# One probability tile per head, V products by key block, and the softmax sums inverted late and sent through DRAM

## The chip, the cores and the metric

The kernel runs on one core of a Trainium2 chip. The metric is the device time of one execution in microseconds (us), lower is better. The engines are named as in the profile: PE (TensorE matmul), PEld (its weight loads), DVE (VectorE), ACT (ScalarE), POOL (GpSimd) and SP (SyncE, which here issues all DMAs of the program from one queue, in order).

## The reference

Two layers over 2048 tokens of width 1024, all float32. Layer A is a gated MLP with spatial gating. Layer B, which the change touches, is chunked band attention with 16 heads of 64 channels: a chunk of 64 queries sees its own chunk and the 8 chunks before it.

```python
def one_chunk(args):
    c, qc = args
    start = c * CHUNK
    kc = lax.dynamic_slice_in_dim(k_pad, start, B_BAND, axis=1)
    vc = lax.dynamic_slice_in_dim(v_pad, start, B_BAND, axis=1)
    sc = jnp.einsum('bqhd,bkhd->bhqk', qc, kc).astype(jnp.float32) + bias
    valid = (m + start) >= B_LEFT_PAD
    sc = jnp.where(valid[None, None, None, :], sc, NEG_INF)
    p = jax.nn.softmax(sc, axis=-1).astype(vc.dtype)
    return jnp.einsum('bhqk,bkhd->bqhd', p, vc)
...
return (o * jax.nn.silu(z)) @ w_out
```

## The kernel before

Matmuls keep float32 accuracy by splitting each operand into a high part, rounded to float32r, and a low part, the rest; a product is two or three matmuls (`mm3`, lines 113 to 115, for the dense layers).

Layer A and the projection of V come first. The attention layer B runs from about 1560 us of the span to the end. It has four token tiles `t` of 512 queries, and in each eight pairs `p` of heads. A head has four query blocks of 128 queries (`qb`), so a pair has eight units, `u` = 0 to 7: head `hd` = u // 4 of the pair, block u % 4. A query block sees five key blocks of 128 keys, 640 keys, in the tiles `t` > 0; in the first tile the keys before the sequence are left out, so it sees 1, 2, 3 or 4 blocks.

A unit goes through three functions:

- `score`: four matmuls (line 1320) into one PSUM tile; DVE adds the bias, negates, and leaves the row minimum (line 1328, tile `pr`); ACT takes the exponential and leaves the row sum in `sl` (line 1335); DVE inverts `sl` (line 1338); POOL multiplies the whole row by it (line 1339).
- `flip`: PE transposes the five blocks of `pr` into the one PSUM tile `tp` (line 1359); ACT copies them as the high part (line 1362) and DVE writes the low part (line 1363) into `pt`. One `pt` tile holds two query blocks side by side, for each of six key blocks: [128, 2 (high, low), 6, 256]. In the first token tile POOL writes zeros into the corner that no block fills (line 1352).
- `value`, once for two query blocks (`g`): the products with V. The stationary operand is a block of V for one head, 64 columns of its high part and 64 of its low part; the moving operand is `pt`, 256 columns at a time. For `t` > 0 there are ten matmuls: eight for the four key blocks that both query blocks see (line 1387), high and low, and one each for the outermost key blocks, in which high and low of one query block stand side by side (lines 1380 and 1381). The two halves of the output are added afterwards: ACT copies one (line 1399), DVE adds the other (line 1401), and for `t` > 0 DVE adds high and low (line 1406). After the last call of a pair DVE multiplies by the gate `zt` (line 1413; for the last two pairs of all `last_og`, line 1486) and the result goes to DRAM.

The order is written out by hand in the loop over `u`, and a scheduler of the framework may still move instructions on each engine within the dependencies. In each step stand: the score of unit u + 2, half of the other work of that step, the flip of unit u, for even u a `value`, and the other half. The other work is a generator (`ahead`): the projection of the next pair (query, key and gate: `pj` tiles), and the output product of the tile before (`bo` tiles). The output product of the last tile stands alone at the end. In the first token tile the projection weights are scaled by the norm gains on POOL (line 184) before ACT and DVE split them (lines 199 and 200). In tiles 0, pairs 2 and 4, POOL also forms sums of the output weights (lines 310 to 319).

The PSUM tiles `tp` and the score tile have one buffer each. SP's queue carries all loads and stores, the shift of the query tiles by 64 partitions (`Qh<-Qh`) among them.

Of the kernel before, what the change touches and what calls it, by code (L numbers as in the profile page):

```python
# [9 lines left out]
F32 = mybir.dt.float32  # L10
F32R = mybir.dt.float32r
# [22 lines left out]
def trunk_kernel(  # L34
# [43 lines left out]
    x2d = [[dram.tile([P, D], F32, name=f"x2d{t}_{b}") for b in range(TB)] for t in range(NT - 1)]  # L78

# [1127 lines left out]
    with ExitStack() as bctx:  # L1207
# [83 lines left out]
        prs = {}  # L1291
        pts = {}
# [12 lines left out]
        def score(t, p, u):  # L1305
# [12 lines left out]
            for i, q in enumerate(qt[t, p, hd]):  # L1318
# [8 lines left out]
            sl = sm.tile([P, 1], F32, tag="sl", name=f"sl{t}_{h}_{qb}", bufs=4)  # L1327
# [8 lines left out]
                pr[:, c0:], pr[:, c0:], AF.Exp, scale=-1.0, bias=nm[:], accum_out=sl[:]  # L1336
            )
            nc.vector.reciprocal(sl[:], sl[:])  # L1338
            nc.gpsimd.tensor_scalar(  # L1339
                pr[:, c0:], pr[:, c0:], sl[:], 1.0, op0=ALU.mult, op1=ALU.mult  # L1340
            )
            prs[t, h, qb] = pr

        def flip(t, p, u):

            hd, qb = divmod(u, 4)
            h = 2 * p + hd
            g, qq = divmod(qb, 2)
            if qq == 0:
                pt = sb.tile([P, 2, 6, 256], F32R, tag="PT", name=f"pt{t}_{h}_{g}", bufs=2)  # L1350
                if t == 0:
                    nc.gpsimd.memset(pt[:, :, 5, 0:P].bitcast(F32), 0.0)
                pts[t, h, g] = pt
            pt = pts[t, h, g]
            pr = prs[t, h, qb]
            b0 = 0 if t > 0 else 4 - qb
            tp = ptr.tile([P, KD, P], F32, tag="tr", name=f"tp{t}_{h}_{qb}")
            for b in range(b0, 5):
                tpose(tp[:, b, :], pr[:, b * P : (b + 1) * P], ident[:])  # L1359
            cs = slice(qq * P, (qq + 1) * P)  # L1360
            oh = pt[:, 0, b0 + qq : 5 + qq, cs]
            nc.scalar.copy(oh, tp[:, b0:5, :])  # L1362
            nc.vector.tensor_tensor(  # L1363
                pt[:, 1, b0 + qq : 5 + qq, cs], tp[:, b0:5, :], oh.bitcast(F32), op=ALU.subtract
            )

        def value(t, p, hd, g):

            h = 2 * p + hd
            pt = pts[t, h, g]  # L1370
            po = pmm.tile([P, 2, 256], F32, tag="mm", name=f"pv{t}_{h}_{g}")
            hs = slice(hd * P, hd * P + P)

            def keys(i):
                return vtl[t, p][:, 2 * g + i, hs]

            if t > 0:
                mm(po[:, :, 0:P], keys(0), pt[:, :, 0, 0:P], start=True, stop=False)  # L1380
                mm(po[:, :, P:256], keys(5), pt[:, :, 5, P:256], start=False, stop=False)
                blocks = range(1, 5)
            else:
                blocks = range(4 - 2 * g, 6)
            for j in range(2):
                for i in blocks:
                    mm(  # L1387
                        po[:, 0, :], keys(i), pt[:, j, i, :],
                        start=(t == 0 and j == 0 and i == blocks[0]),
                        stop=(j == 1 and i == blocks[-1]),  # L1390
                    )
            if hd == 0 and g == 0:
                og32s[t, p] = sb.tile([P, T], F32, tag="og32", name=f"og32_{t}_{p}", bufs=1)
            og32 = og32s[t, p]
            r, r2 = halves(hd)
            ot = sb.tile([P, 2, 256], F32, tag="ot", name=f"ot{t}_{h}_{g}", bufs=1)
            oq = og32[r, g * 256 : (g + 1) * 256]
            n = 2 if t > 0 else 1
            nc.scalar.copy(ot[r, :n, :], po[r2, :n, :])
            o1 = ot[r, :, :] if t > 0 else oq  # L1400
            nc.vector.tensor_tensor(
                o1, po[r, :n, :] if t > 0 else po[r, 0, :],
                ot[r, :n, :] if t > 0 else ot[r, 0, :], op=ALU.add,
            )
            if t > 0:
                nc.vector.tensor_tensor(oq, ot[r, 0, :], ot[r, 1, :], op=ALU.add)
            if g == 0:
                return
            if hd == 1 and t + 1 == NT and p >= 6:
                last_og(p, og32, zt[t, p])  # L1410
            elif hd == 1:
                og = sb.tile([P, T], F32, tag="og", name=f"og{t}_{p}", bufs=2)
# [220 lines left out]
        for t in range(NT):  # L1633
            for p in range(NPAIR):
# [11 lines left out]
                for u in range(8):  # L1646
# [6 lines left out]
                    done = max(done, upto)  # L1653
                    flip(t, p, u)
# [15 lines left out]
        value(*before, 1, 1)  # L1670
# [61 lines left out]
```

## Time and profile before

| | |
|---|---|
| median of 3 runs | 2727.69 us (2720.04 to 2733.72) |
| the profiled execution, its own time | 2731.61 us |
| its span in the profile | 2728.6 us |
| mean granted TensorE clock | 0.986 |
| PE busy | 2630.1 us, 96% |
| DVE busy | 1961.0 us, 72% |
| ACT busy | 1324.8 us, 49% |
| POOL busy | 909.8 us, 33% |

Busy times of PE overlap, since a matmul starts while the one before it drains: what a matmul costs in a dense stretch is the distance from its start to the next start, which the timeline shows. In the groups of instructions, the number after the bar is idle time of that engine just before the group, with what ended it.

### The profile page before, as it was taken

To read this page: it belongs to the slowest core of one execution; us is meant where nothing else is said; L and a number is where in the kernel's file an instruction comes from. 1 tells how busy PE (TensorE), PEld (TensorE's weight loads), DVE (VectorE), ACT (ScalarE), POOL (GpSimd) and SP (SyncE) were. 2 spreads that over 40 slices of the span, in tenths; PEclk is the share of its full clock that TensorE was granted. 3 is DMA by queue.
4 is the path that set the end of the run, shared out by engine and by line. 5 is a ranking of instruction groups with operands and counts; after the bars stand their busy time and mean duration, and the time that the engine had idled before them with its cause. 6 is when DMAs were issued, how large, how long until landed. Compare 5 with 4: busy or idle time off the path is not lost. (4 is left out here: it accounts for less than half of the span.)

```text
span 2728.6 us, 38857 instructions
## 1 busy us (share of the span) xinstructions
PE 2630.1 (96%) x13216; PEld 2199.9 (81%) x13216; DVE 1961.0 (72%) x3097; ACT 1324.8 (49%) x2360; POOL 909.8 (33%) x906
## 2 busy tenths in 40 slices
PE   8999999999999999999989998999999999999997
PEld 7888888888888888888867776778887888788885
DVE  5655676676676669666677776677788778877787
ACT  5422242433424445332455465566656666666554
POOL 3512236142251414115143344322333223323243
PEclk9999999999999999999999999899999999999999
DMA  7899999989888879668667787766777667865567
GB/s 297 314 326 335 345 358 327 329 306 349 333 300 295 302 263 342 236 236 308 239 219 277 238 274 249 243 211 208 234 253 246 219 211 238 264 203 192 185 228 251
DMA packets 274773, 735.56 MB, mean 270 GB/s; under 512 B 29584, under 2 KB 61328, under 8 KB 274576
## 3 DMA queue, kind: packets, MB, share of 16 engines
q1 hardware_dynamic: 274576, 733.09, 77.9%
q8 instruction: 105, 1.72, 0.3%
q14 instruction: 92, 0.75, 0.1%
HBM read 540.56 MB, written 181.93 MB: 265 GB/s over the span
## 5 line engine op out<-in xcount | busy, mean ns | idle before, releaser
L113 PE MATMUL P<-T,S 128*128 128x512 f32 x1248 | 496.1, 398 | 2.7 <-ACT S L376 2.0
L115 PE MATMUL P<-T,S 128*128 128x512 f32 x1248 | 490.3, 393 | 0.0
L114 PE MATMUL P<-T,S 128*128 128x512 f32 x1248 | 489.1, 392 | 1.1 <-DVE T L379 1.1
L1339 POOL TENSOR_SCALAR pr<-pr,sl 128x640 f32<-128x640 f32 (+4 forms) x256 | 202.8, 792 | 553.9 <-DVE sl L1338 512.8
L113 PE MATMUL pj<-hh_b,wh_b 128*128 128x512 f32 x768 | 316.8, 412 | 7.7 <-ACT wh_b L199 6.7
L114 PE MATMUL pj<-hl_b,wh_b 128*128 128x512 f32 x768 | 307.4, 400 | 0.0
L115 PE MATMUL pj<-hh_b,wl_b 128*128 128x512 f32 x768 | 306.5, 399 | 0.0
L1335 ACT ACTIVATE pr<-pr,nm 128x640 f32<-128x640 f32 (+4 forms) x256 | 195.3, 763 | 222.4 <-DVE nm L1328 217.5
L115 PEld LDWEIGHTS P<-T,S 128*128 128x128 f32 x1248 | 235.4, 189 | 50.3
L113 PEld LDWEIGHTS P<-T,S 128*128 128x128 f32 x1248 | 235.9, 189 | 48.1 <-ACT S L376 2.3
L114 PEld LDWEIGHTS P<-T,S 128*128 128x128 f32 x1248 | 235.8, 189 | 46.9 <-DVE T L379 1.3
L1363 DVE TENSOR_TENSOR pt<-tp,pt 128x640 fp32r<-128x640 f32 (+4 forms) x256 | 188.8, 738 | 75.4 <-ACT pt L1362 73.1
L1328 DVE CUSTOM_DVE_ANT_0 pr<-s,bias 128x640 f32<-128x640 f32 (+4 forms) x256 | 188.2, 735 | 21.4 <-PE s L1320 15.6
L1362 ACT CAST pt<-tp 128x640 fp32r<-128x640 f32 (+4 forms) x256 | 158.6, 620 | 60.8 <-PE tp L1359 58.0
L1359 PEld LDWEIGHTS tp<-ident,pr 128*128 128x128 f32 x1120 | 135.1, 140 | 54.5 <-POOL pr L1339 15.9
L1359 PE MATMUL tp<-ident,pr 128*128 128x128 f32 x1120 | 165.8, 274 | 12.7 <-DVE pt L1363 6.5
L115 PEld LDWEIGHTS pj<-hh_b,wl_b 128*128 128x128 f32 x768 | 147.3, 192 | 32.6
L113 PEld LDWEIGHTS pj<-hh_b,wh_b 128*128 128x128 f32 x768 | 147.7, 192 | 27.5 <-ACT wh_b L199 8.3
L114 PEld LDWEIGHTS pj<-hl_b,wh_b 128*128 128x128 f32 x768 | 147.9, 193 | 17.3 <-issue 0.2
L1387 PE MATMUL pv<-pt,V 128*128 128x256 f32 x960 | 143.0, 289 | 11.2 <-ACT pt L1362 11.1
L200 DVE TENSOR_TENSOR wl_b<-raw_b,wh_b 128x1024 fp32r<-128x1024 f32 x96 | 122.9, 1280 | 42.4 <-ACT wh_b L199 41.2
L1387 PEld LDWEIGHTS pv<-pt,V 128*128 128x128 f32 x960 | 127.5, 193 | 14.9 <-ACT pt L1362 13.6
(291 smaller groups left out, 5941.5 us busy)
## 6 DMA issues: line engine op xcount, KB each, us to landing
S<-hsd SPq DMA_DIRECT2D x288, 512.0 KB, 5.5
rw<-in_w_a SPq DMA_DIRECT2D x108, 512.0 KB, 6.5
A<-ytd SPq DMA_DIRECT2D x72, 512.0 KB, 5.5
raw_b<-wk SPq DMA_DIRECT2D x72, 512.0 KB, 3.8
hsd<-S SPq DMA_DIRECT2D x56, 512.0 KB, 4.3
V<-vhd SPq DMA_DIRECT2D x56, 512.0 KB, 5.0
wh_bo<-ows SPq DMA_DIRECT2D x50, 512.0 KB, 4.5
wl_bo<-ows SPq DMA_DIRECT2D x50, 512.0 KB, 5.6
```

The source lines that it names most:

```text
L113: first = mm(ps, lh, rh, start=first, stop=False)
L114: mm(ps, lh, rl, start=False, stop=False)
L115: mm(ps, ll, rh, start=False, stop=last)
L200: tv(wl[:], raw[:], wh[:].bitcast(F32), op=sub)
L1328: nc.vector.tensor_tensor_reduce(out=pr[:, c0:].rearrange("p (a b) -> p a b", a=nseg), in0=ps[:, :nseg, :w], in1=bias[:, c0:].rearrange("p ...
L1335: nc.scalar.activation(pr[:, c0:], pr[:, c0:], AF.Exp, scale=-1.0, bias=nm[:], accum_out=sl[:])
L1339: nc.gpsimd.tensor_scalar(pr[:, c0:], pr[:, c0:], sl[:], 1.0, op0=ALU.mult, op1=ALU.mult)
L1359: tpose(tp[:, b, :], pr[:, b * P : (b + 1) * P], ident[:])
L1362: nc.scalar.copy(oh, tp[:, b0:5, :])
L1363: nc.vector.tensor_tensor(pt[:, 1, b0 + qq : 5 + qq, cs], tp[:, b0:5, :], oh.bitcast(F32), op=ALU.subtract)
L1387: mm(po[:, 0, :], keys(i), pt[:, j, i, :], start=(t == 0 and j == 0 and i == blocks[0]), stop=(j == 1 and i == blocks[-1]),)
```

## The change

The probabilities are no longer multiplied by the inverse sums. The eight row sums of a pair go into eight columns of one tile; DVE inverts that tile once, after the eighth exponential. PE transposes it, 128 x 8 to 8 x 128, into a free slot of the `tp` tile of unit 6 (unit 5 in the last pair of all). ACT copies the 8 x 128 to SBUF, one DMA writes it to DRAM, two DMAs read it back, each spread over the 64 partitions of a head, and POOL multiplies the result by the gate.

One `pt` tile holds all four query blocks of a head, and has one buffer. `value` is called once for a head and goes by key block: for each of the eight key blocks (four in the first token tile) two matmuls, high and low, over all query blocks that see it, so 128, 256, 384 or 512 columns. High and low are accumulated in one PSUM tile, and the output is read once for a head. `value` of the first head stands ahead of the flip of unit 4, that of the second ahead of the flip of unit 0 of the next pair; the gate and the store follow in `gated`, one step later.

```diff
-            sl = sm.tile([P, 1], F32, tag="sl", name=f"sl{t}_{h}_{qb}", bufs=4)
+            if u == 0:
+                sums[t, p] = sm.tile([P, 8], F32, tag="sl", name=f"sl{t}_{p}", bufs=2)
...
             nc.scalar.activation(
-                pr[:, c0:], pr[:, c0:], AF.Exp, scale=-1.0, bias=nm[:], accum_out=sl[:]
+                pr[:, c0:], pr[:, c0:], AF.Exp, scale=-1.0, bias=nm[:],
+                accum_out=sums[t, p][:, u : u + 1],
             )
-            nc.vector.reciprocal(sl[:], sl[:])
-            nc.gpsimd.tensor_scalar(
-                pr[:, c0:], pr[:, c0:], sl[:], 1.0, op0=ALU.mult, op1=ALU.mult
-            )
+            if u == 7:
+                nc.vector.reciprocal(sums[t, p][:], sums[t, p][:])
...
-                pt = sb.tile([P, 2, 6, 256], F32R, tag="PT", name=f"pt{t}_{h}_{g}", bufs=2)
-                if t == 0:
-                    nc.gpsimd.memset(pt[:, :, 5, 0:P].bitcast(F32), 0.0)
+            if qb == 0:
+                pts[t, h] = sb.tile([P, 5376], F32R, tag="PT", name=f"pt{t}_{h}", bufs=1)
...
             for b in range(b0, 5):
                 tpose(tp[:, b, :], pr[:, b * P : (b + 1) * P], ident[:])
+            if u == sums_at(t, p):
+                tpose(tp[0:8, 5, :], sums[t, p][:], ident[:])
...
+            if u == sums_at(t, p):
+                inverse(t, p, tp[0:8, 5, :])
+
+        def sums_at(t, p):
+            return 5 if t + 1 == NT and p + 1 == NPAIR else 6
+
+        def inverse(t, p, src):
+            rc = sm.tile([8, P], F32, tag="rc", name=f"rc{t}_{p}", bufs=1)
+            nc.scalar.copy(rc[:], src)
+            nc.sync.dma_start(rcd[t][p].rearrange("(a b) -> a b", b=P), rc[:])
+            w = zt[t, p, 1] = sb.tile([P, T], F32, tag="og", name=f"w{t}_{p}", bufs=2)
+            for hd in range(2):
+                nc.sync.dma_start(
+                    w[hd * 64 : hd * 64 + 64, :],
+                    rcd[t][p, hd * T : hd * T + T].partition_broadcast(64),
+                )
+            tg(w[:], w[:], zt[t, p][:], op=ALU.mult)
 
-        def value(t, p, hd, g):
+        def value(t, p, hd):
...
+            blocks = (3, 4, 0, 1, 2, 5, 6, 7) if t > 0 else (4, 5, 6, 7)
+            for i in blocks:
+                q0, q1 = max(0, i - 4), min(4, i + 1)
+                for j in range(2):
+                    o = j * 2560 + q0 * 512 + i * P
+                    rhs = pt[:, o : o + P]
+                    if q1 - q0 > 1:
+                        rhs = pt[:, o : o + (q1 - q0) * 512].rearrange("p (q c) -> p q c", c=512)
+                        rhs = rhs[:, :, 0:P]
                     mm(
+                        po[:, q0 * P : q1 * P], vtl[t, p][:, i, hs], rhs,
+                        start=(i == blocks[0] and j == 0), stop=(i == 7 and j == 1),
                     )
...
+            nc.scalar.copy(ot[r, :], po[r2, :])
+            nc.vector.tensor_tensor(og32[r, :], po[r, :], ot[r, :], op=ALU.add)
+
+        def gated(t, p):
+            og32, og = og32s[t, p], zt[t, p, 1]
+            if t + 1 == NT and p >= 6:
+                last_og(p, og32, og)
+            else:
                 nc.vector.scalar_tensor_tensor(
-                    og[:], og32[:], 0.5, zt[t, p][:], op0=ALU.mult, op1=ALU.mult
+                    og[:], og32[:], 0.5, og[:], op0=ALU.mult, op1=ALU.mult
                 )
...
+                    if u == 1 and before:
+                        gated(*before)
+                    if u == 4:
+                        value(t, p, 0)
+                    elif u == 0 and before:
+                        value(*before, 1)
                     flip(t, p, u)
...
-                    if u % 2 == 0:
-                        if u:
-                            value(t, p, *divmod(u // 2 - 1, 2))
-                        elif before:
-                            value(*before, 1, 1)
...
-        value(*before, 1, 1)
+        value(*before, 1)
+        gated(*before)
```

More of the change, by code (lines that the diff above doesn't have):

```diff
@@ L78, in trunk_kernel @@
     x2d = [[dram.tile([P, D], F32, name=f"x2d{t}_{b}") for b in range(TB)] for t in range(NT - 1)]
+    rcd = [dram.tile([NPAIR, 8 * P], F32, name=f"rcd{t}") for t in range(NT)]
     reld = [dram.tile([P * 768], F32, name=f"reld{h}") for h in range(NH)]
@@ L1291, in trunk_kernel @@
         prs = {}
+        sums = {}
         pts = {}
@@ L1367, in value @@
-        def value(t, p, hd, g):
+                pt[:, 2560 + o + b0 * P : 2560 + o + 640],
+                tp[:, b0:5, :].rearrange("p a b -> p (a b)"), oh.bitcast(F32), op=ALU.subtract,
+            )
+            if u == sums_at(t, p):
[13 more added lines that the diff above has]
+            tg(w[:], w[:], zt[t, p][:], op=ALU.mult)
@@ L1369, in value @@
+        def value(t, p, hd):
             h = 2 * p + hd
-            pt = pts[t, h, g]
-            po = pmm.tile([P, 2, 256], F32, tag="mm", name=f"pv{t}_{h}_{g}")
+            pt = pts[t, h]
+            po = pmm.tile([P, T], F32, tag="mm", name=f"pv{t}_{h}")
             hs = slice(hd * P, hd * P + P)
[L1374 to L1390, printed above, removed]
-                    )
-            if hd == 0 and g == 0:
-                og32s[t, p] = sb.tile([P, T], F32, tag="og32", name=f"og32_{t}_{p}", bufs=1)
+            blocks = (3, 4, 0, 1, 2, 5, 6, 7) if t > 0 else (4, 5, 6, 7)
@@ L1394, in value @@
+            if hd == 0:
+                og32s[t, p] = sb.tile([P, T], F32, tag="og32", name=f"og32_{t}_{p}", bufs=2)
             og32 = og32s[t, p]
             r, r2 = halves(hd)
[L1396 to L1412, printed above, removed]
+            ot = sb.tile([P, T], F32, tag="ot", name=f"ot{t}_{h}", bufs=1)
+            nc.scalar.copy(ot[r, :], po[r2, :])
+            nc.vector.tensor_tensor(og32[r, :], po[r, :], ot[r, :], op=ALU.add)
```

12 lines of the change are left out of this document (4 added, 8 removed).

## The prediction

> **What bounds the kernel now.** I read the busy times first (PE 96% of the span, in the table above), then a table of stretches of layer B, then who PE waits for where it is not full. The columns of the stretches are their length, the busy time and instructions of PE, PEld, DVE, ACT and POOL, the granted clock, the busy share of the DMA engines and GB/s.
>
> ```profile
> 1560.00:1810.00 250.00, 221.44 (x1111) 179.85 (x1110) 169.33 (x398) 144.63 (x323) 109.09 (x165) 0.95 0.76 245
> 1810.00:2050.00 240.00, 239.18 (x1376) 207.73 (x1375) 188.41 (x349) 148.46 (x265) 71.89 (x95) 1.00 0.71 231
> 2050.00:2100.00 50.00, 45.05 (x246) 37.66 (x245) 43.07 (x84) 30.83 (x57) 17.56 (x22) 0.93 0.74 241
> 2345.00:2395.00 50.00, 44.98 (x246) 37.47 (x244) 42.83 (x84) 31.09 (x57) 17.66 (x20) 0.93 0.71 229
> 2640.00:2728.00 88.00, 66.43 (x320) 50.38 (x318) 68.07 (x112) 39.82 (x78) 41.92 (x38) 0.97 0.76 259
> ```
>
> Layer B has two regimes. Between 1810 and 2640, PE is full (239.2 of 240) but for two changes of token tile of 50 us, with 5.0 idle in each. There, a microsecond taken from DVE, ACT or POOL is worth nothing, and one added to PE is a microsecond. In the first token tile (1560 to 1810) PE is idle for 28.6 us, and its granted clock is 0.95, which is another 0.05 x 250 = 12.5 us lost. At the end 21.6 of 88 are idle. So the sum has a term in PE work and a term in waits.
>
> The waits of the first token tile, of PE, of POOL and of ACT:
>
> ```profile
> PE pv L1387 <- ACT pt L1362: 11.1, 5, 4.2
> PE s L1320 <- DVE nm L1328: 3.5, 3, 2.2
> PE tp L1359 <- DVE pt L1363: 3.5, 7, 0.9
> PE tp L1359 <- POOL pr L1339: 3.2, 1, 3.2
> ```
> ```profile
> POOL pr L1339 <- DVE sl L1338: 94.9, 55, 4.4
> POOL pt L1352 <- PE pv L1387: 21.2, 13, 4.0
> ACT wh_b L199 <- POOL raw_b L184: 20.0, 8, 5.0
> ```
>
> The columns are total us, times and the longest. The largest, V products waiting for ACT's copy of the transposes, is not ACT being busy. The timeline shows the worst one:
>
> ```profile
> 1670.81 0.63 PE L1387 MATMUL pv<-pt,V 128*128 128x256 f32 x3 [4.24 <-ACT pt L1362]
> 1667.86 1.04 ACT L199 CAST wh_b<-raw_b 128x1024 fp32r<-128x1024 f32 x1 [5.04 <-POOL raw_b L184]
> ```
>
> ACT, in order, stood 5.04 us for weights that POOL had yet to scale; the copy for PE was queued behind. And POOL, in order too, spends its time standing at the normalization (94.9 us) and at the zeroing (21.2). Both go with this change.
>
> **PE work.** A dense stretch gives the price of each width as the distance between starts:
>
> ```profile
> 1893.16 0.36 PE L1380 MATMUL pv<-pt,V 128*128 128x256 f32 x1
> 1893.36 0.28 PE L1381 MATMUL pv<-pt,V 128*128 128x256 f32 x1
> 1893.48 1.12 PE L1387 MATMUL pv<-pt,V 128*128 128x256 f32 x8
> 1894.44 0.40 PE L113 MATMUL pj<-hh_b,wh_b 128*128 128x512 f32 x1
> 1894.67 0.40 PE L114 MATMUL pj<-hl_b,wh_b 128*128 128x512 f32 x1
> 1897.80 0.71 PE L1359 MATMUL tp<-ident,pr 128*128 128x128 f32 x5
> 1898.26 0.48 PE L113 MATMUL pj<-hh_b,wh_b 128*128 128x512 f32 x1
> 1898.58 0.40 PE L114 MATMUL pj<-hl_b,wh_b 128*128 128x512 f32 x1
> 1901.71 0.71 PE L1359 MATMUL tp<-ident,pr 128*128 128x128 f32 x5
> ```
> ```profile
> 1607.52 0.34 PE L1320 MATMUL s<-K,Qh 128*128 128x384 f32 x1
> 1607.70 0.35 PE L1320 MATMUL s<-K,Ql 128*128 128x384 f32 x1
> 1607.89 0.40 PE L113 MATMUL pj<-hh_b,wh_b 128*128 128x512 f32 x1
> ```
> ```profile
> 1659.48 0.22 PE L1320 MATMUL s<-K,Qh 128*128 128x128 f32 x1
> 1659.54 0.28 PE L1320 MATMUL s<-K,Ql 128*128 128x128 f32 x1
> 1659.65 0.45 PE L113 MATMUL pj<-hh_b,wh_b 128*128 128x512 f32 x1
> 1659.93 0.39 PE L114 MATMUL pj<-hl_b,wh_b 128*128 128x512 f32 x1
> ```
>
> 512 columns cost 0.23 (1894.44 to 1894.67), 256 cost 0.12 (eight in 0.96), 384 cost 0.185. Two of 128 and the 512 after them take 0.45 (1659.48 to 1659.93), so 0.11 for each 128: the first start comes after 0.06, but the next two gaps are stretched. The first matmul after transposes pays 0.08 or 0.09 more (0.20 at 1893.16, 0.32 at 1898.26), one for each flip, before and after the change.
>
> Both forms stream 5120 columns for a head in the later tiles. Before: 20 matmuls of 256, 20 x 0.12 = 2.40. After: four each of 512, 384, 256 and 128, so 0.92 + 0.74 + 0.48 + 0.44 = 2.58. That is +0.18 for a head and, for 48 heads, +8.6 us: the narrow ends cost more than the wide middle saves. In the first token tile 12 of 256 (1.44) become two of each width (1.29): -0.15 x 16 = -2.4. The transposed sums are one more transpose for each of 32 pairs; five take 0.46, so 0.09 x 32 = +2.9. PE work in all: **+9.1 us**, nearly all where PE is full.
>
> By the Trainium skill's "TensorE: Matmul & The Clock Gate", section "Back-to-back issue gap", a matmul of N columns costs N/2.4 + 2.5 ns, so the head would go from an estimated 2.18 us to 2.17 and the change would add nothing there. The same page's section "LDWEIGHTS (loading the stationary operand)" speaks against the change: 128 columns of weights take 128/1.2 = 107 ns to load, whatever the moving width. The rows' second gap, 0.11, agrees with the latter; the first, 0.06, with the former.
>
> **What the other engines lose and gain.** Rows of the later tiles (DVE), then of the first (POOL), and two kinds of DMA (KB each, us to landing):
>
> ```profile
> L1401 DVE TENSOR_TENSOR ot<-pv,ot 64x512 f32<-64x512 f32 x91 | 62.3, 685 | 8.0 <-ACT ot L1399 6.6
> L1406 DVE TENSOR_TENSOR og<-ot 64x256 f32<-64x256 f32 x91 | 40.8, 448 | 2.6
> L1338 DVE RECIPROCAL sl<-sl 128x1 f32<-128x1 f32 x181 | 28.9, 160 | 61.3 <-ACT pr L1335 60.2
> L1339 POOL TENSOR_SCALAR pr<-pr,sl 128x128 f32<-128x128 f32 (+2 forms) x68 | 41.8, 615 | 95.1 <-DVE sl L1338 94.9
> L1437 POOL TENSOR_TENSOR A_s<-A,A 128x512 f32<-128x512 f32 x2 | 3.0, 1503 | 0.0
> Qh<-Qh SPq DMA_DIRECT2D x64, 128.0 KB, 4.1
> ogd<-og SPq DMA_DIRECT2D x60, 128.0 KB, 3.0
> ```
>
> A later pair loses on DVE seven reciprocals (1.1), two reads of PSUM (1.4) and four adds (1.8), 4.3 us, with the standing at ACT in front of each reciprocal. POOL loses eight multiplications of a row and gains one product of 1.5. ACT loses two copies and gains one of 8 x 128. In the full stretches all this is hidden already and earns nothing.
>
> *First token tile.* I count the 3.2 on POOL as gone, half of the 11.1 (the part that POOL's lateness makes; the rest is weights arriving from DRAM), and half of the 7.0 that DVE causes: 12.2 of 28.6 idle. With it goes that share of the lost clock, 12.5 x 12.2/28.6 = 5.3. Together **-17.5**; the bounds are 0 (another chain is late next: load, scaling, split) and -41 (all idle and all lost clock). I take a value nearer to the middle because half of the named waits lead back to POOL or DVE.
>
> *Changes of token tile.* DVE is 86% busy there; a pair takes 36 us (four steps of 3.9, 1897.80 to 1901.71, and four with a `value`, 1.28 more), so 50 hold 1.4 pairs, which lose 6 us of it. I take **-3** of the 10 idle (0 to -10).
>
> *End.* The last head's V products now all stand behind the last flip: 1.3 us (the half head of 1893.16 to 1894.44) moves behind it, with less DVE work after. **+1** (-3 to +4).
>
> **New waits, and why I price them at nothing.** (1) `value` needs the low part of the flip just before it, with one `pt` buffer. From that flip to `value` PE has 3.9 us of other work (1897.80 to 1901.71). The slowest flip of the dense stretches is the one ahead of a change of tile:
>
> ```profile
> 2053.98 0.71 PE L1359 MATMUL tp<-ident,pr 128*128 128x128 f32 x5
> 2057.52 0.81 DVE L1363 TENSOR_TENSOR pt<-tp,pt 128x640 fp32r<-128x640 f32 x1
> 2058.48 0.30 PE L1359 MATMUL tp<-ident,pr 128*128 128x128 f32 x1
> ```
>
> Its low part is done after 4.35 us, and PE came for its next flip after 4.50. It fits, narrowly; up to 0.15 for each of 64 heads, 10 us, is the upper bound. (2) The inverse sums: a step is 3.9 or 5.2 us. From unit 6 to `gated`, three steps on, is some 13. The way takes, with the two DMA rows as bounds from larger transfers, a copy (an estimate of 0.5, below the 0.685 of DVE's 64x512), 3.0 for the write, 4.1 for the reads and 1.5 on POOL, 9.1. It fits unless queues are long. On SP the two reads stand for the write's landing, about 3 us, with weight and key loads queued behind; on POOL the product stands for the reads, with bias masks, residual sums and, in the first tile, weight scaling behind it. In the later tiles PE's cover is the queued loads being early; in the first it is thin.
>
> **Sum.** 9.1 - 17.5 - 3 + 1 = -10.4 against the profiled execution's 2731.6: 2721.2. That execution stood 3.9 above the median of the runs, 2727.7, so the forecast is **2717**. What a measurement of this kernel can tell from no change is about 0.5%, 13.6 us: faster is under 2714, slower over 2741.
>
> **Rivals.**
> *Nothing comes back.* In the first tile the load of weights, 20.0 us of ACT standing for `raw_b` included, is late for DRAM's sake. Then 9.1 + 1 remain: 2738. For: DMA is 0.76 busy there. Against: POOL stood 116 us at the two steps that go. Chance 0.22.
> *Slower: the round trip blocks POOL.* In each pair of the first tile POOL reaches the gate product before the reads have landed, weight scaling waits behind it, ACT behind that, and PE as in the 4.24 us shown: 8 x 4.2 = 34, with 9.1: 2771. It decides once POOL is some 2 us early in most pairs, since PE has lost 4.24 where ACT stood 5.04. Against: POOL has 30 us less to do there (41.8 less eight products of 1.5). Chance 0.14.
> *Columns alone count.* If a 128 costs its first gap, 0.06, a head costs 2.38, -1.0 for the later tiles, -4.0 in the first, +2.9 for sums: 11 us under the forecast, 2706. The issue-gap rule of the Trainium skill's "TensorE: Matmul & The Clock Gate" would have it so (section "Back-to-back issue gap"). Against: the stretched gaps. Chance 0.12.
> *All idle of the first tile and the tile changes goes:* 9.1 - 41 - 10 + 1, 2687. Against: DMA arrivals stay. Chance 0.10.
>
> **How the numbers follow.** The forecast has 0.42; its own range is 2708 to 2727 (9 either way in the first tile), and 0.13 of it lies under 2714. Faster: 0.13 + 0.12 + 0.10 = 0.35. Slower: 0.14, and 0.06 of the first rival with the 10 us of late flips: 0.20. Same: 0.45. The range runs from 2692 to 2748 (2738 and those 10); left out are the blocked POOL and half of the last rival, 0.19.
>
> **What would show it.** Right: V products of 128 columns some 0.11 apart and a dense pair 0.45 us longer; PE full from 1810 on; in the first tile fewer than 18 us idle and POOL without its long standing. Wrong: PE waiting at `pv` for DVE's low parts in dense stretches; POOL or DVE standing at the reads; or 128s at 0.06.

## The result

| | before | after |
|---|---|---|
| median of 20 runs | 2724.12 us (2716.94 to 2733.72) | 2734.90 us (2730.00 to 2736.71) |
| the profiled execution, its own time | 2731.61 us | 2731.47 us |
| its span | 2728.6 us | 2729.7 us |

The ratio is 1.0034, with a 95% interval from 1.0027 to 1.0042: the change costs 0.34%, some 9 us, under the 0.5% that was called no change. A second measurement in another session gave 1.0026 (1.0013 to 1.0039; `after_again` below). The forecast was 2717, 7 us under the median of before's 20 runs; the change goes the other way.

The stretches of the changed kernel that answer to those shown of before, with the same columns (length, busy time of PE, PEld, DVE, ACT and POOL, granted clock, DMA share, GB/s):

```profile
1560.00:1810.00 250.00, 223.24 (x1073) 177.07 (x1073) 171.45 (x328) 149.06 (x323) 70.75 (x75) 0.95 0.78 256
1810.00:2050.00 240.00, 238.47 (x1313) 206.29 (x1313) 161.75 (x261) 140.77 (x257) 36.81 (x49) 1.00 0.73 237
2050.00:2100.00 50.00, 46.30 (x264) 39.75 (x263) 42.74 (x73) 31.79 (x60) 9.11 (x13) 1.00 0.80 262
2345.00:2395.00 50.00, 47.45 (x259) 40.48 (x259) 41.85 (x69) 31.41 (x58) 10.06 (x13) 0.97 0.78 251
2640.00:2728.00 88.00, 64.90 (x277) 49.14 (x275) 57.50 (x88) 34.71 (x67) 33.66 (x29) 0.90 0.68 242
```

POOL is relieved as planned (109 to 71 in the first token tile, 72 to 37 in the dense stretch). DVE is relieved in the dense stretch (188 to 162), but not in the first tile (169 to 171). PE has hardly come closer to full in the first tile (26.8 idle, 28.6 before), and its clock there is 0.95 as before. The end is worse: 23.1 of 88 idle, and the clock went from 0.97 to 0.90.

To put the microseconds in places, I cut each profile at the first score step on DVE of certain pairs (numbered 0 to 31 through the four token tiles), the same points in every kernel. "Dense" is pairs 7 to 15, 17 to 23 and 25 to 31; "changes" is 15 to 17 and 23 to 25; "end" begins with pair 31. Each kernel was profiled three times in all:

| us | to pair 7 | dense | changes | end | span |
|---|---|---|---|---|---|
| before, three profiles | 1767.9, 1762.0, 1766.9 | 715.5, 718.1, 717.8 | 148.7, 147.4, 149.3 | 96.5, 96.4, 95.7 | 2728.6, 2723.8, 2729.7 |
| after, three profiles | 1762.1, 1761.5, 1764.5 | 721.8, 722.4, 721.7 | 140.9, 141.2, 143.0 | 104.9, 103.9, 104.2 | 2729.7, 2729.0, 2733.5 |
| difference of the means | -2.9 | +4.9 | -6.8 | +8.2 | +3.4 |

The dense stretches, the changes and the end repeat within a few microseconds, and each differs between the kernels by more than it scatters. The first stretch scatters by 6. The three profiles put the difference at 3.4 us where the medians have 7 to 11. Which executions were profiled is a part of that: the first profiled execution of before (2731.6) stands 7.5 above the median of its kernel's 20 runs, the first two of the changed kernel stand 3.4 and 6.5 under theirs. So some 4 us or more of the difference is not in these tables, and in which stretch it lies is open.

The waits of the first token tile in the changed kernel (total us, times, longest), for PE and for POOL, and POOL's row for the whole span:

```profile
PE tp L1357 <- DVE pt L1363: 7.6, 10, 1.8
PE s L1322 <- DVE nm L1331: 6.1, 5, 2.3
PE pj L114 <- ACT wh_b L200: 6.0, 4, 2.4
...
PE tp L1357 <- ACT rc L1376: 2.2, 2, 1.2
```
```profile
POOL bias L1303 <- DMA bias<-reld: 64.2, 15, 13.4
POOL raw_b L185 <- DMA raw_b<-in_w_kqz: 44.4, 7, 14.8
POOL w L1384 <- DMA w<-rcd: 29.1, 6, 8.8
```
```profile
POOL w L1384 <- DMA w<-rcd: 123.0, 25, 11.0
```

V products waiting for ACT's copies, 11.1 us before, are gone from the head of PE's list. In their place PE stands longer for DVE (7.0 to 13.7), for weights (6.0, before 1.9), and for ACT's copy of the transposed sums, a wait that before did not have. POOL no longer stands at the normalization but at loads: for the inverses 29.1 us in the first tile, 123.0 in all. The timeline shows one round trip and what queues behind it:

```profile
1701.19 0.28 SPq L1377 DMA_DIRECT2D rcd<-rc  x1
...
1703.78 1.90 POOL L185 TENSOR_TENSOR raw_b<-raw_b,bg 128x1024 f32<-128x1024 f32 x1 [14.81 <-DMA raw_b<-in_w_kqz]
...
1705.70 0.32 SPq L213 DMA_DIRECT2D wk<-raw_b  x1
...
1706.12 1.20 SPq L1380 DMA_DIRECT2D w<-rcd  x2
...
1707.37 0.58 SPq L1299 DMA_DIRECT2D bias<-reld  x1
1707.99 0.91 SPq L211 DMA_DIRECT2D raw_b<-in_w_kqz  x2
...
1710.07 1.28 POOL L1384 TENSOR_TENSOR w<-w,Z 128x512 f32<-128x512 f32 x1 [4.40 <-DMA w<-rcd]
1711.73 0.14 POOL L1303 MEMSET bias<- 64x64 f32 x1 [0.37 <-DMA bias<-reld]
1711.90 0.29 DVE L1331 CUSTOM_DVE_ANT_0 pr<-s,bias 128x128 f32<-128x128 f32 x1 [3.89 <-POOL bias L1303]
```

From write to reads 4.9 us pass on SP. Most of it is not the write's landing, for which SP stood twice in this tile, 4.7 us in all: the store of scaled weights (`wk<-raw_b`) stands ahead of the reads in SP's order, and it waits until POOL has scaled them at 1705.68, which POOL could not do before their load. Behind the reads the bias and two weight loads are issued. POOL stands 4.40 for the reads, then does the product; behind it stands the mask of the next bias tile, and DVE stood 3.89 us for that mask before it could do a score step. But the mask stood another 0.37 after the product for its own load, so here the load, issued behind the reads on SP, set the time, and not the product.

The same holds for all eight products of the first tile in each of the three profiles of the changed kernel. Behind 15 of the 24 products, POOL's next step waited on for its own load (0.26 to 3.44 us); behind the other nine it began at once, and no engine is seen to stand for it. POOL's 29.1 us are a long wait, but these traces do not show that they delay PE.

The end, PE's waits from 2640 to 2728, and what each of three standstills is followed by. The timeline rows have in brackets how long PE stood; the rows below them are the 7 us after each, with the granted clock as the third number from the end:

```profile
PE bo L114 <- ACT wh_bo L200: 4.2, 2, 3.9
PE tp L1357 <- DVE pt L1363: 3.2, 3, 1.6
PE bo L115 <- DVE wl_bo L201: 2.8, 3, 1.2
PE bo L115 <- DMA wl_bo<-ows: 1.8, 2, 1.4
PE tp L1357 <- ACT rc L1376: 1.8, 1, 1.8
```
```profile
2658.63 0.77 PE L1357 MATMUL tp<-ident,pr 128*128 128x128 f32 x5 [1.80 <-ACT rc L1376]
2661.04 1.33 PE L1357 MATMUL tp<-ident,pr 128*128 128x128 f32 x5 [1.64 <-DVE pt L1363]
...
2711.41 0.80 PE L114 MATMUL bo<-wh_bo,Sho 128*128 128x512 f32 x1 [3.95 <-ACT wh_bo L200]
```
```profile
2658.60:2665.60 7.00, 4.55 (x16) 3.43 (x17) 3.48 (x7) 1.38 (x2) 0.55 (x1) 0.58 0.85 290
2661.00:2668.00 7.00, 6.18 (x25) 5.11 (x25) 2.13 (x3) 0.69 (x1) 0.00 (x0) 0.61 0.89 276
2711.40:2718.40 7.00, 5.97 (x15) 4.29 (x16) 4.71 (x8) 0.90 (x1) 1.48 (x1) 0.55 0.39 150
2677.00:2684.00 7.00, 7.00 (x32) 5.59 (x30) 3.25 (x6) 3.42 (x7) 1.28 (x1) 1.00 0.76 283
```

The first two standstills come close together, at one flip (the copy of the sums) and the next (its low part), and after them the clock is at 0.58 and 0.61; after the third it is 0.55; between them, where PE is full, it is 1.00. At a lower clock the same matmul takes longer: from 1708.66 to 1710.79, at a granted clock of 0.50, products of 512 columns start 0.43 us apart, and from 1711.02 on, at 1.00, 0.23 apart. So 7 us at 0.55 lose an estimated 3 where PE has work. Before was idle nearly as long at its end (21.6 us), but in smaller pieces, 1.71 us the longest, and kept a clock of 0.97.

### The profile page after: what moved, and what is told of

It reads as the page before. It is cut to its first block, busy times and chain, and to the rows that moved or that the text cites. A ratio compares the mean times of both kernels' runs of the same rounds, so it can differ in the third digit from the quotient of the medians.

```text
span 2729.7 us, 37466 instructions
## 1 busy us (share of the span) xinstructions
PE 2633.2 (96%) x12992; PEld 2196.4 (80%) x12992; DVE 1874.1 (69%) x2713; ACT 1301.2 (48%) x2328; POOL 744.1 (27%) x650
## 5 line engine op out<-in xcount | busy, mean ns | idle before, releaser
L114 PEld LDWEIGHTS pj<-hh_b,wh_b 128*128 128x128 f32 x768 | 146.6, 191 | 27.9 <-ACT wh_b L200 8.9
L1303 POOL MEMSET bias<- 64x64 f32 x64 | 9.3, 145 | 577.5 <-DMA bias<-reld 506.4
L1401 PEld LDWEIGHTS pv<-pt,V 128*128 128x128 f32 x896 | 144.6, 190 | 18.5 <-ACT pt L1362 2.6
L1401 PE MATMUL pv<-pt,V 128*128 128x256 f32 (+3 forms) x896 | 154.9, 321 | 1.6 <-ACT pt L1362 1.3
```

The lines of the kernel that those rows point to most:

```text
L114: first = mm(ps, lh, rh, start=first, stop=False)
L1303: nc.gpsimd.memset(bias[0:64, 576:640], NEG)
L1401: mm(po[:, q0 * P : q1 * P], vtl[t, p][:, i, hs], rhs, start=(i == blocks[0] and j == 0), stop=(i == 7 and j == 1),)
```

## The experiments

All ratios are against runs of the kernel before on the same chip in the same session. Theory at the start: the change is two things, and the way of the inverses through DRAM costs what the freed engines give. Rivals: the V products by key block cost it (PE's narrow blocks, or products late behind the last flip).

**`products_alone`**: products by key block from one `pt` tile per head, the old normalization.

```diff
-                accum_out=sums[t, p][:, u : u + 1],
+                accum_out=sl[:]
+            nc.vector.reciprocal(sl[:], sl[:])
+            nc.gpsimd.tensor_scalar(pr[:, c0:], pr[:, c0:], sl[:], 1.0, op0=ALU.mult, op1=ALU.mult)
...
-            if u == sums_at(t, p):
-                tpose(tp[0:8, 5, :], sums[t, p][:], ident[:])
-                inverse(t, p, tp[0:8, 5, :])
```

> One half of the change: one pt tile per head and V products by key block, but each row is normalized at once as before (reciprocal and POOL multiplication for every unit, gate from zt without a round trip). Theory A (the added time is PE work, and the first tile gives nothing back because its weights arrive late): PE work +8.6 in the later tiles and -2.4 in the first, less what DVE's lost reads give back at the changes of tile, so +2 to +7 us against the kernel before. Theory B (the round trip of the inverse sums takes back what the freed POOL gave): without the round trip this half is no slower than before by more than 1 us, or faster.

Measured: 0.9977 (0.9967 to 0.9986), 6 us *faster* than before. Changes of tile 142.3, as in the changed kernel; dense stretches 718.3, hardly above before's mean of 717.1; end 101.4.

**`sums_alone`**: the counterpart, the old products and `pt` tiles with the late sums.

```diff
-            nc.vector.reciprocal(sl[:], sl[:])
-            nc.gpsimd.tensor_scalar(pr[:, c0:], pr[:, c0:], sl[:], 1.0, op0=ALU.mult, op1=ALU.mult)
+            if u == 7:
+                nc.vector.reciprocal(sums[t, p][:], sums[t, p][:])
...
+            if u == sums_at(t, p):
+                tpose(tp[0:8, 5, :], sums[t, p][:], ident[:])
+                inverse(t, p, tp[0:8, 5, :])
```

> The other half: sums inverted once, transposed, through DRAM, into the gate; products with V by two query blocks from the double-buffered pt tile as before (og32 keeps one buffer). Theory A: PE work +2.9, some 5 us back at the two changes of tile, some 5 lost at the last pair where the sums' copy holds the transposes, so -2 to +4 us. Theory B: the round trip costs the same as in the whole change, so +8 us or more.

Measured: 1.0072 (1.0056 to 1.0088), 20 us slower. The changes of tile stay as in before (149.1), the end is 104.7, the dense stretches 724.0. So the half with the products is a gain, the half with the sums is the loss, and the gain at the changes belongs to the products. The halves do not add up: -6 and +20 make 14, the whole change has 7 to 9 by its ratios. What joins them is open.

**`no_round_trip`**: the sums are inverted, transposed, copied and written, but neither read back nor multiplied.

```diff
-            w = zt[t, p, 1] = sb.tile(...)
-            for hd in range(2):
-                nc.sync.dma_start(w[hd * 64 : hd * 64 + 64, :], rcd[t][p, ...].partition_broadcast(64))
-            tg(w[:], w[:], zt[t, p][:], op=ALU.mult)
```

> The changed kernel without the way back: the sums are inverted, transposed, copied and written to DRAM, but not read, and POOL does not multiply the gate, so the division by the sums is left out of the output. Theory A: the reads and the product on POOL cost little, 0 to 4 us less than the changed kernel, so +7 to +10 against the kernel before. Theory B: POOL's standing at the reads (29 us in the first tile) is what holds weights and bias masks back, so at least 9 us less than the changed kernel, level with the kernel before or below.

Measured: 0.9992 (0.9979 to 1.0004), 9 to 11 us under the changed kernel; the stretch to pair 7 took 1753.4, the end 100.0. So the way back is what puts the change above before. The late sums gain nothing even without it: `products_alone`, which normalizes each row, has 0.9977 in the same session.

**`last_pair_old`**: the changed kernel with the very last pair normalized the old way.

```diff
+            own = t + 1 == NT and p + 1 == NPAIR
+            if own:
+                nc.vector.reciprocal(sl[:], sl[:])
+                nc.gpsimd.tensor_scalar(pr[:, c0:], pr[:, c0:], sl[:], 1.0, op0=ALU.mult, op1=ALU.mult)
...
-            return 5 if t + 1 == NT and p + 1 == NPAIR else 6
+            return 8 if t + 1 == NT and p + 1 == NPAIR else 6     # never for the last pair
```

> The changed kernel, but the very last pair normalizes each row at once as before, so that no sums are transposed, copied or sent in it. In the profile of the changed kernel the stretch from the first score of the last pair to the end is 8 us longer than before, with PE standing 1.8 us for the copy of the sums and 1.6 for the low part after it. Theory A: this part is worth 4 to 8 us, so +3 to +7 against the kernel before. Theory B (the end is longer because all V products of the last head stand behind the last flip): no change from the changed kernel, +9 to +12.

Measured: 1.0014 (1.0006 to 1.0023), 3 to 5 us under the changed kernel, which is Theory A's number; but the end is 106.6, no shorter, so its profile does not show the gain where the theory has it. It tells little: a normalization of the last pair stood on POOL behind 9.4 us of sums of the output (`A_hl`, 2639.33 to 2648.75), and PE stood 5.78 us for it. One trouble was exchanged for another.

**`after_again`**: the changed kernel, as a control beside the next three.

> The changed kernel as it is, on the chip of the runs beside it, so that their ratios have one to stand against. From its first measurement, 1.0034 of the kernel before (+9 us), with the first token tile at about 198 us (pairs 0 to 7, from the first score step of one to that of the other) and the end at about 105 us after the last pair's first score step. If it comes within 0.1% of 1.0034, ratios of different calls may be set side by side.

Measured: 1.0026 (1.0013 to 1.0039). The two ratios of the changed kernel lie 0.0008 apart and their intervals overlap. Where a ratio of another session is set beside it below, both are used.

**`product_on_dve`**: the gate product moves from POOL to DVE, ahead of the gate's step; SP's queue stays as it is.

```diff
-            tg(w[:], w[:], zt[t, p][:], op=ALU.mult)     # in inverse
+            nc.vector.tensor_tensor(w[:], w[:], zt[t, p][:], op=ALU.mult)     # one pair later, before gated
```

> The gate product stands on DVE, just ahead of the gate's own step one pair later, in place of POOL just behind the reads; write and reads stay as they are on SP. Leaving the round trip out had given back some 12 us (ratio 0.9992 against 1.0034). Theory POOL: POOL's standing at the reads (123 us in all, bias masks and weight scaling behind it) is what costs. Then most of it comes back here: 8 to 10 us under the changed kernel (ratio 0.9995 to 1.0005), the first token tile at about 190 us. Rival SP: the loads queued behind the two reads on SP are what is late. Then nothing comes back: within 2 us of the changed kernel, the first token tile at about 198 us, POOL's standing now at raw_b in the whole.

Measured: 1.0005 (0.9992 to 1.0017), medians 7.9 us apart from `after_again` in the same session. By the medians, having the product on POOL is the larger part of the cost, and not the reads on SP. How it costs is not shown. The profile is only 2.2 us shorter (end 101.1 against 103.9, to pair 7 1760.3 against 1761.5), since the profiled execution of `after_again` was 6 us under its median. The first token tile took 195.2, not about 190, and PE stood 4.8 us there for weights (`wh_b`), as in the three profiles of the changed kernel (4.7 to 6.0). Where the reads are gone too it stood 1.8 (`no_round_trip`) and 3.4 (`no_trip_first_tile`). That speaks for a share of SP's in this tile.

**`trip_on_pool_queue`**: as `product_on_dve`, and the write and reads are issued from POOL's queue.

```diff
-            nc.sync.dma_start(rcd[t][p]..., rc[:])     # and both reads
+            nc.gpsimd.dma_start(rcd[t][p]..., rc[:])
```

> As product_on_dve, and the write and the two reads are issued from POOL's queue in place of SP's, so that nothing stands behind them on SP, while POOL stands for the copy of the inverses and for the write's landing, about 3 us for each pair. Theory POOL: POOL still stands, for less; half of the 12 us comes back at most, and product_on_dve is the faster of the two by 2 us or more. Rival SP: the loads come earlier; 8 us or more under the changed kernel, the first token tile at about 190 us, and faster than product_on_dve by 6 us.

Measured: 1.0206 (1.0184 to 1.0227), 56 us slower, much more than either theory had. POOL's timeline, then DVE's wait (whole span) and PE's (1810 to 2640):

```profile
1914.53 0.14 POOL L1303 MEMSET bias<- 64x64 f32 x1 [16.05 <-DMA bias<-reld]
1914.71 0.15 POOL L1304 MEMSET bias<- 64x64 f32 x1
1919.58 0.54 POOL L1377 DMA_DIRECT2D rcd<-rc  x1 [4.71 <-ACT rc L1376]
1921.61 1.29 POOL L1447 TENSOR_TENSOR A<-A,A 128x512 f32<-128x512 f32 x1 [1.50 <-DMA rcd<-rc]
1922.86 1.07 POOL L1380 DMA_DIRECT2D w<-rcd  x2
```
```profile
DVE w L1388 <- DMA w<-rcd: 70.3, 23, 7.5
```
```profile
PE tp L1357 <- DVE pt L1363: 28.3, 18, 3.5
```

The issues now stand in POOL's order, behind masks that wait 16 us for a bias load; the reads come so late that DVE stands 70.3 us at the product, and the low parts of the flips stand behind it. Here the trip costs what stands in order behind each of its waits. Whether SP's part could be had back in a cleaner way stays open.

**`halves_at_end`**: `products_alone`, with the last head's products in two halves of 256 queries, one of them two flips earlier.

```diff
+                    elif u == 6 and t + 1 == NT and p + 1 == NPAIR:
+                        value(t, p, 1, 0)
...
-        value(*before, 1)
+        value(*before, 1, 1)
```

> The products by key block with the old normalization (products_alone, 0.9977), and the very last head's V products in two halves of 256 queries, the first of them two flips earlier, as the kernel before has it. In products_alone the end took 101.4 us against 96.5 before. Theory: this lengthening is the products that all stand behind the last flip; with the halves the end is back at 96 to 98 us and the time 3 to 5 us under products_alone (ratio 0.996 to 0.9967). Rival: the end is set by the output weights' loads and the chain behind the gate; then the end stays at 100 to 102 us and the ratio at 0.9977 within 0.0006.

Measured: 0.9981 (0.9970 to 0.9992), no gain, and the end 105.0, longer than the rival's 100 to 102. Taking the products from behind the last flip does not shorten the end; the rival holds in that.

**`no_trip_first_tile`** and **`no_trip_later_tiles`**: the reads and the product left out in the first token tile, and in the three later ones.

```diff
+            if t == 0:     # t > 0 in the other
+                return
             w = zt[t, p, 1] = sb.tile(...)
```

> The changed kernel with the two reads and the gate product left out for the first token tile alone (its division is left out of the output); the sums are still inverted, transposed, copied and written. Over all tiles this had given 12 us (no_round_trip). Theory: the first tile, where POOL also scales the weights, takes most of it: 7 to 10 us under the changed kernel (ratio 0.9995 to 1.0005 against 1.0026 to 1.0034), the first tile at 189 to 192 us. Rival: it is the end, where three standstills of PE with a lower clock behind them stand; then no more than 3 us come back here, and the first tile stays at 196 to 198.

Measured: 1.0000 (0.9988 to 1.0011), 7 to 9 us under the changed kernel, with the first token tile at 191.7 and the end at 106.4.

> The counterpart: reads and product left out for the three later token tiles alone. Theory: 2 to 5 us under the changed kernel (ratio 1.001 to 1.0025), all of it at the end, which goes from 104 to about 100 us; the first tile stays at 197. Rival: 9 us or more (0.9997 or less), if the end or the dense stretches carry it. The two gains together should come near 12 us.

Measured: 1.0015 (1.0005 to 1.0025), 3 to 5 us under it, with the end at 99.7. Its profile is of the slowest of its 12 executions, with the first tile at 202.3, not 197. The two add up to the 9 to 11 of the whole within their intervals: some two thirds of the trip's price is paid in the first token tile, the rest in the later ones, and of these the profiles show it at the end.

**`no_narrow_blocks`**: the products of 128 columns left out.

```diff
-            blocks = (3, 4, 0, 1, 2, 5, 6, 7) if t > 0 else (4, 5, 6, 7)
+            blocks = (3, 4, 1, 2, 5, 6) if t > 0 else (4, 5, 6)
```

> The changed kernel without the V products of 128 columns (first and last key block of each head; their part is left out of the output): 4 for each head of the later tiles, 2 in the first, 224 in all. Theory of the prediction: a 128 costs 0.11 us, so 24.6 us in all, of which what lies where PE is full, 192 x 0.11 = 21, must come back: ratio 0.992 to 0.9955. Rival, columns alone: 0.06 each, 11.5 to 13.4 us: 0.998 to 0.9992.

Measured: 0.9985 (0.9975 to 0.9995), 11 to 13 us, the rival's number; but the stretches say that the number is no price. Dense fell from 722.0 to 706.5 and the changes from 141.7 to 134.6, 22.6 us together, what the theory has (21). The stretch to pair 7 rose from 1762.7 to 1774.2. A head's products, changed kernel and this one:

```profile
2178.68 2.66 PE L1401 MATMUL pv<-pt,V 128*128 128x512 f32 x16
2181.17 0.73 PE L1357 MATMUL tp<-ident,pr 128*128 128x128 f32 x5
```
```profile
2181.43 2.24 PE L1401 MATMUL pv<-pt,V 128*128 128x512 f32 x12
2183.51 0.71 PE L1357 MATMUL tp<-ident,pr 128*128 128x128 f32 x5
```

2.49 less 2.08 is 0.41 for four, 0.10 each. And the first tile of this kernel:

```profile
PE pj L114 <- ACT wh_b L200: 13.7, 6, 4.1
```

With some 3 us less work (32 products of 0.10) PE stands more than twice as long for weights there (6.0 in the changed kernel), and the tile took 210.6 us, 8 to 14 more than in the changed kernel's three profiles. So in this one profile less PE work gains nothing in the first tile; why the weights come later was not followed.

**`last_pair_on_dve`**: `products_alone`, with the very last pair normalized on DVE.

```diff
+            norm = nc.vector if t + 1 == NT and p + 1 == NPAIR else nc.gpsimd
-            nc.gpsimd.tensor_scalar(
+            norm.tensor_scalar(
```

> Products by key block with the old normalization (products_alone, 0.9977), and the very last pair's normalization on DVE in place of POOL. In products_alone PE stood 3.66 us at its end for a normalization that POOL had queued behind sums of the output, and for 7 us after it the granted clock was 0.76. Theory: both go, 3 to 5 us: ratio 0.996 to 0.9967, the end at 96 to 98 us against 101.4. Rival: DVE is the engine that is late there (69 of 101 us busy), PE stands for its low parts instead and nothing comes back: 0.9977 or above.

Measured: 0.9968 (0.9955 to 0.9980), 2721.78 us against 2728.60, faster than both kernels; the end is 99.1 against 101.4. Above the wait at the end of `products_alone` that it removes, below the longest that it has in its place:

```profile
PE tp L1357 <- POOL pr L1341: 3.7, 1, 3.7
```
```profile
PE tp L1358 <- DVE pt L1362: 3.6, 2, 2.3
```

The intervals of the two overlap, so that it beats `products_alone` is likely, not shown.

**`before_second_look`, `before_third_look`, `after_third_look`**: the two kernels as they are, for further profiles.

> The kernel before as it is, for a second profile. Theory: its first token tile (pairs 0 to 7) varies from run to run with the weights' arrival; here it takes 190 to 197 us, not 200.8, and the end stays at 96 to 97. Rival: it is 200 to 202 again; then the rest of the difference of the medians lies in the part ahead of the attention, which is the same code in both.

> The kernel before as it is, for a third profile; as for the second one.

> The changed kernel as it is, for a third profile. Theory: the first token tile at 197 to 200 us, the dense stretches at 283.3 to 284, 222 and 216.7 us, the end at 104 to 105, as in its two profiles so far.

Measured: they are in the table of the result. From the first score step of pair 0 to that of pair 7 before took 200.8, 194.7 and 198.8 us, the changed kernel 197.9, 197.0 and 202.9. So the first tile varies by 6 us from run to run in either kernel, and neither expectation is met by all. The idle time does not: before has 28.6, 27.9 and 28.0 us of it from 1560 to 1810. The clock does, 0.95, 0.97 and 0.95.

## Why the prediction was wrong

*PE work, predicted +9.1: right in kind, a third too high.* The narrow product costs what was said (0.104, from heads of 2.492 and 2.075, against 0.11). Inside a head its four starts lie 0.06, 0.11, 0.07 and 0.11 apart, and the 256 behind the first two takes 0.17 in place of 0.12: a short distance is paid for later, so both readings of the rows were right and the price is the longer one. But the head as a whole is 2.49 against two runs of ten of 1.27, of which 0.08 is the step after transposes: 2.38. That is +0.11 for a head, not +0.18, since the sum of 2.58 was put together from rounded distances of other rows, where the run as a whole is 2.49. For 48 heads it is 5.2 instead of 8.6, and PE work in all some +5.7. The dense stretches, 20 of the pairs, grew by 4.9; 20 x (0.22 + 0.09) is 6.2. Of the 4.9 some 2 belong to the products: with them and the old normalization these stretches took 718.3, 719.4 and 720.1 (`products_alone`, `halves_at_end`, `last_pair_on_dve`), 717.1 in the mean before. That is half of 20 x 0.22, and where the other half is gained is open. The other 3 belong to the sums: their transposes, and 2.3 us in which PE's next flip stands for ACT's copy. By the Trainium skill's "TensorE: Matmul & The Clock Gate", section "Back-to-back issue gap", a 128 would cost an estimated 56 ns by the formula, which the section gives for a matmul in isolation; for a stream with weight loads it has some 81 ns. The Trainium skill's section "LDWEIGHTS (loading the stationary operand)" there has 107 ns by its formula, and the measured 104 agrees with that.

*Changes of token tile, predicted -3 (0 to -10): the right sign, -6.8.* In before two standstills follow each other at each change (2.39 and 2.01 us, then 2.40 and 2.01), and the clock behind the second is 0.58 to 0.80 in its three profiles, at the first change of the first one:

```profile
2068.40:2075.40 7.00, 6.99 (x23) 5.70 (x24) 5.02 (x13) 1.60 (x4) 4.04 (x6) 0.58 0.97 309
```

After it there is one at each, of 2.55 to 2.95 us, with 0.76 to 1.00 behind; the 50 us after 2050 have a clock of 1.00, those after 2345 of 0.97. The prediction counted the idle time there and not the clock behind it.

*First token tile, predicted -17.5 with -2.4 of PE work and the sums' +0.7: the step that failed.* The mean of the profiles to pair 7 is -2.9, where -19 was forecast, and even that lies ahead of pair 0: from its first score step to that of pair 7 the changed kernel takes 199.3 us in the mean, before 198.1. Two things went wrong. First, the step counted 12.2 us of named waits as gone, with their share of the clock: the 3.2 at POOL's normalization whole, and half of the waits for ACT's copies and for DVE. V products did stop waiting for ACT, but PE then stood at DVE's steps and at weights for about as long; DVE was no less busy in this tile (169 and 171). With the round trip left out the tile took 189.1 (`no_round_trip`) and 191.7 (`no_trip_first_tile`), 6 to 9 under before's mean: the relief is worth less than half of what was forecast.

Second, new wait (2), the round trip, was priced at nothing. Its 9.1 us were set against the 13 until `gated`, its own user, and that comparison held (DVE stood 2.6 to 4.8 us in all for the gate product). What stands behind the trip on SP and on POOL was named, but it got no term in the sum, and it takes 7 to 9 us back in this tile. The rival "the round trip blocks POOL" had the price at 34. Its condition came true, POOL stood up to 8.8 us at six of the eight products; but what stood behind them was mostly waiting for its own loads as well. Whether the 7 to 9 come through POOL or through the loads behind the reads on SP is not settled: the medians of `product_on_dve` speak for POOL, the waits for weights in the profiles for SP.

*End, predicted +1: +8.2.* The prediction moved 1.3 us of products and looked no further. `halves_at_end` shows no gain from those. What costs is shown in part. Leaving out the trip takes 4 to 5 off (100.0 and 99.7). With it goes the longest standstill above: PE stands 3.9 us for `wh_bo` in each of the three profiles of the changed kernel and in `no_trip_first_tile`, not at all in `no_round_trip` and `no_trip_later_tiles`, and 0.7 in `product_on_dve`. It is not the only way to a long end: `no_narrow_blocks` has the trip and 105.2 without that wait.

The copy of the sums makes PE stand 1.80 us, the low part behind it 1.64, with the clock at 0.58 and 0.61. The transposed sums lie in the one PSUM tile of the transposes, so PE's next flip waits for ACT's copy of the inverses too, a wait the prediction did not list. `no_round_trip` keeps that copy and is still 4 longer than before: PE is idle for no longer there (21.5 of 100.0, before 22.2 of 96.6), but its clock is 0.92 against 0.97, which makes an estimated 5 us. That the copy is the whole reason is not shown: `products_alone` has no sums and an end 5 longer than before, there with a wait of its own, for a normalization late on POOL (3.7).

*New wait (1)* was rightly priced at nothing: PE's V products waited 0.2, 0.2 and 1.3 us in all for low parts in the three profiles.

*The sum.* By stretches the change is -2.9 + 4.9 - 6.8 + 8.2 = +3.4 in the profiles; the medians have 7 to 11, and the difference stays open.

## What to carry to other kernels

A trip through DRAM is not free because its result comes in time: give what stands in order behind each of its waits a term in the sum, on the queue that issues it and on the engine that first touches the result. Here an engine that touched the result only where it was needed was the better place, by 7.9 us. When half of a change frees an engine that does not bound, look for the half that relieves the one in front of PE and try the halves singly: here one half gains 6 us and the other takes that and more. Where PE waits now for one thing and now for another, a wait that goes is not yet a saving, since the next one takes its place (here 11.1 us at ACT's copies went, and DVE and the weights took as much); take such a term at its lower end.

## What the runs showed of the chip

A standstill of PE mostly costs more than its length. In the six profiles of the two kernels there are 71 standstills over 1.5 us in layer B; in 52 of them the granted clock of the 7 us behind was under 0.9, mostly 0.55 to 0.8, which is an estimated 1.4 to 3 us more where PE has work. Not all: before's first change has 0.58, the changed kernel's 1.00 behind 2.71 us. Two standstills within 2 us of each other were always followed by a low clock (0.51 to 0.80). The value 0.76 comes most often, 20 times.

The Trainium skill's "TensorE: Matmul & The Clock Gate", section "Part 1: The HAM clock gate (the "warmup" mystery)", says that the clock is either whole or half, and is set by how busy PE was in a free-running window of some 3.4 us. The 0.76 agrees with one such window at half clock (3.4 of 7 us, an estimated 0.76), and that the same standstill is sometimes followed by nothing agrees with the free running. The Trainium skill's section "HAM oscillation — how this bites in real kernels" there warns of gaps over 3.4 us; the rows here show the lower clock behind 1.64 to 2.4 us already, and the measurement decides.

DMAs issued from POOL's queue are no way around SP's: with some three quarters of POOL's time free, the same three transfers of each pair cost 55 us more there than from SP (1.0206 against 1.0005). The rows above show them standing in POOL's order, behind a mask that waited 16.05 us for its load.
